# Element-wise sums and products of a fused 256-token network moved from GpSimd to the Vector Engine, in pieces

## The chip, the cores and the metric

The kernel runs on one core of one Trainium2 chip. The core has five engines that work through separate queues of instructions: TensorE for matrix products (PE in the profile; its weight loads are PEld), VectorE (DVE), ScalarE (ACT), GpSimd (POOL) and SyncE (SP), which here only issues DMAs. They wait for each other by semaphores. The metric is the time on the device of one execution, in microseconds (us); lower is better.

## The reference

256 tokens of width 2048 pass through two blocks. The first block is an S5 state-space mixer and a block-sparse attention (NSA), each with a residual and a layer norm; the second block holds two linear recurrences (HGRN2 and a gated delta rule) and a layer of 16384 experts (PEER). Cut to what the change touches:

```python
x = layer_norm(ALPHA * x + s5_mixer(x, ...), ln_g[0], ln_b[0])   # first norm
shared = shared_kv(x, kv_w, ...)                                 # keys, values: x @ kv_w
x = layer_norm(ALPHA * x + nsa_mixer(x, ..., shared), ln_g[1], ln_b[1])   # second norm
xn = _rmsnorm(x, attn_norm_g)
# HGRN2, per chunk: decay between two positions t and s of a chunk
diff = b_c[..., :, None, :] - b_c[..., None, :, :]               # cumulated log decays
att = einsum('bhtd,bhsd,bhtsd->bhts', q_c, k_c, exp(where(causal, diff, -inf)))
h = x + mix @ w_out
hn = _rmsnorm(h, ffn_norm_g)
# PEER, 8 heads
v1, i1 = top_k(s1, 16); v2, i2 = top_k(s2, 16)
cand = v1[..., :, None] + v2[..., None, :]
best, pos = top_k(cand, 16)                                      # pos over the 16 x 16 sums
expert = take_along_axis(i1, pos // 16) * 128 + take_along_axis(i2, pos % 16)
```

## The kernel before, in words

The program is one long chain of stages: `s5`, the first norm (`ln_hat`), `attention`, the second norm (`ln_rms`), `mixers` (gated delta rule and `hgrn`), a third norm (`rms_channels` alone), and `peer`. All weights stream in through one object, `Stream`, in slabs of 128x1024 numbers: SP issues a DMA into one of three `raw` buffers, ACT rounds it to a coarser form `wh` (L152), and a subtraction on DVE yields the rest `wl = raw - wh` (L153). TensorE multiplies the tokens with `wh` and `wl`; three `wh`/`wl` pairs exist. A `wl` that is late stops TensorE. In the first norm's stage a slab feeds 24 products of 256 columns, in `peer` 8 pairs of a 512-column and a 256-column product (tile `pu`).

The order of each engine's queue is fixed when the program is built: a scheduler of the tile framework picks it, and `issue_after(x)` forbids an instruction to stand ahead of x. At run time each queue is worked through in that order, and an instruction that waits holds all behind it.

The places that the change touches:

- First norm. `ln_hat` leaves the normalised tokens both for the product and, in `res`, for the residual. The residual still wants gain and bias: `affine` (L785) multiplies and adds over 128x2048 for each half of the tokens, on POOL (L789, L790), with `gain` (L732) loading both rows from `ln`, spread over 128 partitions. Meanwhile TensorE makes the keys, tile `pk`, eight `kT` tiles, copied out by ACT and DVE by turns (L815).
- Second norm. `ln_rms` applies mean, scale, gain and bias in pieces of 512 columns: five of eight as two DVE instructions (L689, L690), three as ACT Identity (L692) and two POOL instructions (L694, L695). ACT squares each piece, and `rms_channels` scales by the root mean square: half 0 of the tokens on ACT for the first two quarters and DVE for the others (L721, L723), half 1 on DVE (L724). Then TensorE turns the result over (tile `ptc`).
- `rms_channels` also prepares one weight slab on POOL (`prep(2, gpsimd)`) in the second and the third norm.
- `hgrn`. Seven levels l = 6 to 0: differences `E` of the cumulated logs (L1402, POOL, 128x2048), two exponentials on ACT, products with k and q on DVE (L1405, L1406), small matrix products (tile `hp`, L1422), a masked copy into `att` (L1425). TensorE fills the time in between with a projection (tile `pz`).
- `top` finds the best 16 of 128 keys twice per head and forms 16x16 sums, `cand` (L1456, POOL), for a third search on DVE. `routing` compares positions with a ramp (`eq`, L1486, DVE), multiplies with the indices (L1490, POOL, 128x2048) and sums (L1493, DVE). Both run as background steps: one step for every `pu` tile of the expert products.

Of the kernel before, what the change touches and what calls it, by code (L numbers as in the profile page):

```python
# [14 lines left out]
AF = mybir.ActivationFunctionType  # L15
OP = mybir.AluOpType
# [4 lines left out]
T, D = 256, 2048  # L21
# [148 lines left out]
class Kern:  # L170
# [505 lines left out]
    def ln_rms(self, gb, scale):  # L676

        v, act, gp = self.nc.vector, self.nc.scalar, self.nc.gpsimd
        x = self.ln_x
        st = [self.ln_stats(t) for t in range(2)]  # L680
        out = [self.t8([D]) for _ in range(2)]
        sq = self.small.tile([128, 2, 4], F32, name="lnsq")
        behind = lambda n: self.tc.issue_after(n.ins) if n else ExitStack()
        sqr = None
        for t, q in ((0, 0), (0, 1), (0, 2), (1, 0), (0, 3), (1, 1), (1, 2), (1, 3)):
            c = slice(q * 512, q * 512 + 512)
            o = x[t][:, c]
            if q < 2 + t:
                v.scalar_tensor_tensor(o, o, st[t][0], gb[0][:, c], op0=OP.subtract, op1=OP.mult)  # L689
                dve = v.scalar_tensor_tensor(o, o, st[t][1], gb[1][:, c], op0=OP.mult, op1=OP.add)  # L690
            else:
                act.activation(o, o, AF.Identity, scale=st[t][1], bias=st[t][2])  # L692
                with self.tc.issue_after(self.lastpow) if q == 3 else ExitStack():
                    gp.tensor_tensor(o, o, gb[0][:, c], op=OP.mult)  # L694
                    gp.tensor_tensor(o, o, gb[1][:, c], op=OP.add)  # L695
            with behind(sqr):
                sqr = act.activation(out[t][:, c], o, AF.Square, accum_out=sq[:, t, q:q + 1])
        with self.tc.issue_after(self.lastn):
            self.s.prep(1)
        with behind(sqr), behind(dve):  # L700
            return self.rms_channels(x, out, sq, scale)
# [9 lines left out]
    def rms_channels(self, x, out, sq, scale, alloc=None):  # L711
        v, act = self.nc.vector, self.nc.scalar
        r = self.small.tile([128, 2], F32, name="lnrr")
        for t in range(2):
            v.tensor_reduce(r[:, t:t + 1], sq[:, t], axis=AX.X, op=OP.add)
            self.rstd(r[:, t:t + 1], r[:, t:t + 1], 1e-6, 1, 1.0 / D)
        X, pair = self.channels(out, scale, None, alloc)
        for q in range(4):
            c = slice(q * 512, q * 512 + 512)
            if q < 2:  # L720
                act.activation(out[0][:, c], x[0][:, c], AF.Copy, scale=r[:, 0:1])  # L721
            else:
                v.tensor_scalar(out[0][:, c], x[0][:, c], r[:, 0:1], None, op0=OP.mult)  # L723
            v.tensor_scalar(out[1][:, c], x[1][:, c], r[:, 1:2], None, op0=OP.mult)  # L724
            if q == 0:
                self.s.prep(1)
                with self.tc.issue_after(self.lastpow):
                    self.s.prep(2, self.nc.gpsimd)
            self.pairs(X, pair, q)
        return X  # L730

# [50 lines left out]
            fs.append(lambda k: tiles[k // 4][:, k % 4])  # L782
        return tuple(fs), pair

    def affine(self, eng, x, n):  # L785

        gb = self.gain(n)
        for t in range(2):
            eng.tensor_tensor(x[t], x[t], gb[0], op=OP.mult)  # L789
            eng.tensor_tensor(x[t], x[t], gb[1], op=OP.add)  # L790


    def attention(self, res, X):
# [3 lines left out]
        ident, psum, t8 = self.ident, self.psum, self.t8  # L797
        es = ExitStack()
        P = es.enter_context(self.tc.tile_pool(name="att", bufs=1))
        self.affine(gp, res, 0)  # L800
        mk = P.tile([128, 192], F32, name="mk")
        nc.sync.dma_start(mk, i["masks"])
        cp = t8([320])
# [7 lines left out]
        for n in range(8):  # L811
            ps = psum.tile([128, T], F32, tag="mm", name="pk", bufs=2) if n else self.take_first()
            if n:
                self.mm_b(ps, X)
            (act.copy if n % 2 else v.tensor_copy)(kT[:, n % 4, n // 4, :], ps)  # L815
        vv = t8([2, 2, 512])
        for n in range(2):
            pss = [psum.tile([128, 512], F32, tag=("o", "mm")[n], name="pv", bufs=2) for _ in range(2)]
# [97 lines left out]
        for ci in range(12):  # L916
# [7 lines left out]
            st = {}  # L924
# [450 lines left out]
    def hgrn(self, P, qT, kT, bT, vA, OA, lev):  # L1375
# [19 lines left out]
        for l in range(6, -2, -1):  # L1395
            if l >= 0:
# [2 lines left out]
                blk = lambda x: x.rearrange("p h (n w) -> p (h n) w", w=2 * m)  # L1399
                e, k, q = blk(E), blk(kT), blk(qT)  # L1400
                bb = blk(bT)
                gp.tensor_tensor(e, bb, bb[:, :, m - 1:m].to_broadcast(list(bb.shape)), op=OP.subtract)  # L1402
                act.activation(e[:, :, 0:m], e[:, :, 0:m], AF.Exp, scale=-1.0)
                act.activation(e[:, :, m:], e[:, :, m:], AF.Exp)
                v.tensor_tensor(e[:, :, 0:m], e[:, :, 0:m], k[:, :, 0:m], op=OP.mult)  # L1405
# [31 lines left out]
    def top(self, P, x, c, h):  # L1437
# [14 lines left out]
        for a in range(2):  # L1452
            top16(val[:, h, a], idx[:, h, a], x[:, a, :], tl([128], "tmp1", bufs=2))
            yield 1
        cand = tl([16, 16], "cand", bufs=2)
        self.nc.gpsimd.tensor_tensor(cand, val[:, h, 0, :, None].to_broadcast([128, 16, 16]),  # L1456
                                     val[:, h, 1, None, :].to_broadcast([128, 16, 16]), op=OP.add)
        top16(best[:, h], pos[:, h], cand.rearrange("p a b -> p (a b)"), tl([256], "tmp2", bufs=2))
        yield 1

    def routing(self, P, S):
# [6 lines left out]
        for c in range(2):  # L1468
# [12 lines left out]
            for a in range(2):  # L1481
# [3 lines left out]
                for x in range(0, 128, 64):  # L1485
# [1 line left out]
                                    pf[:, a].rearrange("p h s -> p (h s)")[:, x:x + 64, None].to_broadcast([128, 64, 16]),  # L1487
                                    self.iota16[:, None, :].to_broadcast([128, 64, 16]), op=OP.is_equal)
                    yield 1
                gp.tensor_tensor(eq, eq, idf[:, :, a, None, :].to_broadcast([128, 8, 16, 16]), op=OP.mult)  # L1490
                for x in range(0, 128, 64):
                    yield 1
                    v.tensor_reduce(nn[:, a].rearrange("p h s -> p (h s)")[:, x:x + 64], f[:, x:x + 64, :], axis=AX.X,  # L1493
                                    op=OP.add)
# [544 lines left out]
```

## Time and profile before

| | |
|---|---|
| median of 3 runs | 2997.37 us (2997.36 to 3000.99) |
| the profiled execution | 2999.24 us, span 2997.5 us |
| mean granted TensorE clock | 0.969 |
| PE busy | 2842.1 us, 95% of the span |
| DVE, ACT, POOL busy | 66%, 47%, 20% |

The profile is of one execution. Its span runs from the first to the last instruction; the execution's own time is 1.74 us longer. Times in the trace count from the start of the span. The first norm lies at about 290 to 332 us, the second at 988 to 1021, `hgrn` at 1338 to 1430, the third norm at 1560 to 1580, `top` and `routing` at 1600 to 1850.

### The profile page before, as it was taken

The page shows a single profiled execution, that of the slowest core. Times are in us where ns is not written, and L with a number is a line of the kernel's source. Part 1 is how long each engine was busy: PE and PEld are TensorE (multiplying, and loading weights), DVE is VectorE, ACT ScalarE, POOL GpSimd, SP SyncE. Part 2 cuts the span into 40 slices and gives each one's busy share as a digit, 9 for nine tenths or more (in the row PEclk, how much of TensorE's full clock was granted, in tenths as well). Part 3 has the DMA queues.
Part 4 walks back from the last instruction along what each step waited for, and adds up shares of the span by engine and source line. Part 5 has one row for each costly group of instructions (what it writes and reads, how often), then busy time and mean ns, then how long its engine had stood idle before and what let it go on. Part 6 is the DMA issues. An engine that isn't in the chain of part 4 may idle for free. (4 is left out here: it accounts for less than half of the span.)

```text
span 2997.5 us, 44270 instructions
## 1 busy us (share of the span) xinstructions
PE 2842.1 (95%) x17208; PEld 2492.6 (83%) x17212; DVE 1970.3 (66%) x2991; ACT 1415.3 (47%) x1934; POOL 611.2 (20%) x391
## 2 busy tenths in 40 slices
PE   7889899999999799998999999999989998999996
PEld 7888899988878699987878887888878886888884
DVE  8857644555566766448658898777768544777764
ACT  4365333444444557344444444444434443555553
POOL 4360300000000200013000111000000003888882
PEclk9789999999999899999999999999999998999998
DMA  4235554444456454322565556587875767888883
GB/s 172 71 113 172 173 213 161 156 144 138 155 177 217 142 189 141 113 78 99 190 203 181 173 190 222 176 223 223 222 200 185 213 210 268 299 308 317 315 312 149
DMA packets 232097, 569.52 MB, mean 190 GB/s; under 512 B 84257, under 2 KB 117921, under 8 KB 216002
## 3 DMA queue, kind: packets, MB, share of 16 engines
q1 hardware_dynamic: 173986, 411.46, 42.6%
q0 software_dynamic: 23040, 136.46, 12.6%
q10 hardware_dynamic: 34848, 18.62, 2.0%
q8 instruction: 140, 2.29, 0.3%
q14 instruction: 83, 0.68, 0.1%
HBM read 526.89 MB, written 39.59 MB: 189 GB/s over the span
## 5 line engine op out<-in xcount | busy, mean ns | idle before, releaser
L153 DVE TENSOR_TENSOR wl<-raw,wh 128x1024 fp32r<-128x1024 f32 x685 | 883.6, 1292 | 670.3 <-ACT wh L152 669.3
L152 ACT ACTIVATE wh<-raw 128x1024 fp32r<-128x1024 f32 x688 | 727.0, 1058 | 921.1 <-PE pu L225 220.5
L225 PE MATMUL pu<-h,wh 128*128 128x512 f32 x2048 | 735.8, 400 | 4.8 <-DVE qy L1730 2.9
L226 PE MATMUL pu<-h,wl 128*128 128x256 f32 x2048 | 575.5, 281 | 9.4 <-DVE wl L153 9.4
L225 PEld LDWEIGHTS pu<-h,wh 128*128 128x128 f32 x2048 | 386.8, 189 | 96.8 <-DVE w L1902 4.2
L226 PEld LDWEIGHTS pu<-h,wl 128*128 128x128 f32 x2048 | 387.4, 189 | 11.1 <-DVE wl L153 11.1
L241 PE MATMUL pz<-wh,t 128*128 128x512 f32 x1024 | 336.1, 400 | 0.0
L1808 POOL DMA_INDIRECT wg<-WG,idx x107 | 175.6, 1641 | 704.9 <-DVEq L1948 658.5
L1836 PE MATMUL acc<-vwl,hh 128*128 128x512 f32 x644 | 254.0, 394 | 11.9 <-DVE vwl L177 7.1
L1836 PE MATMUL acc<-vwh,hlo 128*128 128x512 f32 x644 | 250.5, 393 | 0.0
L1836 PE MATMUL acc<-vwh,hh 128*128 128x512 f32 x644 | 225.3, 394 | 14.7 <-ACT vwh L176 14.4
L241 PEld LDWEIGHTS pz<-wh,t 128*128 128x128 f32 x1024 | 192.6, 188 | 40.6 <-issue 1.0
L241 PE MATMUL pz<-wl,t 128*128 128x512 f32 x512 | 201.4, 393 | 1.6 <-DVE wl L153 1.4
L241 PE MATMUL pso<-wh,t 128*128 128x512 f32 x640 | 200.7, 393 | 0.4 <-DVE th L1008 0.4
L177 DVE TENSOR_TENSOR vwl<-h,vwh 128x2048 fp32r<-128x2048 f32 x61 | 139.8, 2292 | 39.6 <-ACT vwh L176 36.4
L1836 PEld LDWEIGHTS acc<-vwh,hh 128*128 128x128 f32 x644 | 122.3, 190 | 41.5 <-ACT vwh L176 14.8
L1836 PEld LDWEIGHTS acc<-vwl,hh 128*128 128x128 f32 x644 | 122.6, 190 | 39.2 <-DVE vwl L177 8.3
L1836 PEld LDWEIGHTS acc<-vwh,hlo 128*128 128x128 f32 x644 | 122.7, 190 | 25.6
L241 PEld LDWEIGHTS pso<-wh,t 128*128 128x128 f32 x640 | 120.2, 188 | 26.8 <-DVE th L1008 0.8
L176 ACT ACTIVATE vwh<-h 128x2048 fp32r<-128x2048 f32 x61 | 116.6, 1912 | 48.3 <-DMA h<-pv,idx 47.6
L212 PE MATMUL pq<-t,wh 128*128 128x256 f32 x768 | 138.1, 283 | 0.0
L1903 ACT ACTIVATE w<-w 128x256 f32<-128x256 f32 x128 | 53.4, 417 | 173.0 <-DVE w L1902 173.0
(621 smaller groups left out, 5325.0 us busy)
## 6 DMA issues: line engine op xcount, KB each, us to landing
raw<-pu SPq DMA_DIRECT2D x256, 512.0 KB, 4.1
raw<-w_z SPq DMA_DIRECT2D x96, 512.0 KB, 3.3
raw<-w_fqi SPq DMA_DIRECT2D x48, 512.0 KB, 3.3
raw<-w_a_in SPq DMA_DIRECT2D x32, 512.0 KB, 3.3
raw<-w_q SPq DMA_DIRECT2D x32, 512.0 KB, 3.3
raw<-w_b_out SPq DMA_DIRECT2D x32, 512.0 KB, 3.9
raw<-w_conv SPq DMA_DIRECT2D x32, 512.0 KB, 3.6
raw<-w_gz SPq DMA_DIRECT2D x32, 512.0 KB, 3.3
```

The source lines that it names most:

```text
L152: self.nc.scalar.activation(h, t, AF.Copy)
L153: m = (engine or self.nc.vector).tensor_tensor(l, t, h.bitcast(F32), op=OP.subtract).ins
L176: self.nc.scalar.activation(h, x, AF.Copy)
L177: (engine or self.nc.vector).tensor_tensor(l, x, h.bitcast(F32), op=OP.subtract)
L212: mm = nc.tensor.matmul(ps, a[:, c], b(k), start=(k == 0 and n == 0), stop=(k == nk - 1 and n == len(ops) - 1))
L225: nc.tensor.matmul(ps, w[0][:, c], x[2](k), start=k == 0, stop=False, skip_group_check=True)
L226: mm = nc.tensor.matmul(ps[:, 0], w[1][:, c], x[0](k), start=False, stop=k == nk - 1, skip_group_check=True)
L241: self.nc.tensor.matmul(pss[tt], x[a](k)[:, ts], b[:, kk * 512:(kk + 1) * 512], start=(k == 0 and n == 0), stop=(k == nk - 1 and n == 2))
L1808: gp.indirect_dma_start(out=g.rearrange("p a b t -> p (a b t)"), out_offset=None, in_=wghalf if a else wgrows, in_offset=off(0))
L1836: m = pe.matmul(acc[t][e], a[:, k], b[:, es], start=start and n == 0, stop=True, skip_group_check=True)
L1903: act.activation(w1, w1, AF.Gelu)
```

## The change

What POOL did in these places is done by DVE, mostly in smaller pieces. In the second norm all eight pieces are DVE pairs, in the order of the tokens' halves, and ACT's Identity goes too. In `rms_channels` ACT scales all of half 0, and the slab that POOL prepared is DVE's. `affine` becomes a generator that does 512 columns of one half per step, one step behind each `kT` tile, not ahead of the last weight slab prepared by then; the loads of gain and bias are issued with the first step; ACT copies all eight `kT` tiles. `hgrn`'s difference is two DVE instructions of 128x1024 per level, `cand` one of 128x256, and the product of `eq` with the indices two of 128x1024, each ahead of a background step.

```diff
@@ ln_rms
-        for t, q in ((0, 0), (0, 1), (0, 2), (1, 0), (0, 3), (1, 1), (1, 2), (1, 3)):
+        for t, q in ((t, q) for t in range(2) for q in range(4)):
             c = slice(q * 512, q * 512 + 512)
             o = x[t][:, c]
-            if q < 2 + t:
-                v.scalar_tensor_tensor(o, o, st[t][0], gb[0][:, c], op0=OP.subtract, op1=OP.mult)
-                dve = v.scalar_tensor_tensor(o, o, st[t][1], gb[1][:, c], op0=OP.mult, op1=OP.add)
-            else:
-                act.activation(o, o, AF.Identity, scale=st[t][1], bias=st[t][2])
-                with self.tc.issue_after(self.lastpow) if q == 3 else ExitStack():
-                    gp.tensor_tensor(o, o, gb[0][:, c], op=OP.mult)
-                    gp.tensor_tensor(o, o, gb[1][:, c], op=OP.add)
+            v.scalar_tensor_tensor(o, o, st[t][0], gb[0][:, c], op0=OP.subtract, op1=OP.mult)
+            dve = v.scalar_tensor_tensor(o, o, st[t][1], gb[1][:, c], op0=OP.mult, op1=OP.add)
@@ rms_channels
-            if q < 2:
-                act.activation(out[0][:, c], x[0][:, c], AF.Copy, scale=r[:, 0:1])
-            else:
-                v.tensor_scalar(out[0][:, c], x[0][:, c], r[:, 0:1], None, op0=OP.mult)
+            act.activation(out[0][:, c], x[0][:, c], AF.Copy, scale=r[:, 0:1])
...
-                    self.s.prep(2, self.nc.gpsimd)
+                    self.s.prep(2)
@@ affine
-    def affine(self, eng, x, n):
+    def affine(self, x, n):
         gb = self.gain(n)
-        for t in range(2):
-            eng.tensor_tensor(x[t], x[t], gb[0], op=OP.mult)
-            eng.tensor_tensor(x[t], x[t], gb[1], op=OP.add)
+        for c in range(0, D, 512):
+            for t in range(2):
+                o = x[t][:, c:c + 512]
+                for g, op in zip(gb, (OP.mult, OP.add)):
+                    self.nc.vector.tensor_tensor(o, o, g[:, c:c + 512], op=op)
+                yield 1
@@ attention
-        self.affine(gp, res, 0)
+        quarters = self.affine(res, 0)
...
-            (act.copy if n % 2 else v.tensor_copy)(kT[:, n % 4, n // 4, :], ps)
+            act.copy(kT[:, n % 4, n // 4, :], ps)
+            with self.tc.issue_after(s.last):
+                next(quarters)
@@ hgrn
-                gp.tensor_tensor(e, bb, bb[:, :, m - 1:m].to_broadcast(list(bb.shape)), op=OP.subtract)
+                nb = 128 // m
+                for x in range(0, 8 * nb, 4 * nb):
+                    r = slice(x, x + 4 * nb)
+                    v.tensor_tensor(e[:, r], bb[:, r], bb[:, r, m - 1:m].to_broadcast([128, 4 * nb, 2 * m]),
+                                    op=OP.subtract)
@@ top
-        self.nc.gpsimd.tensor_tensor(cand, val[:, h, 0, :, None].to_broadcast([128, 16, 16]),
-                                     val[:, h, 1, None, :].to_broadcast([128, 16, 16]), op=OP.add)
+        v.tensor_tensor(cand, val[:, h, 0, :, None].to_broadcast([128, 16, 16]),
+                        val[:, h, 1, None, :].to_broadcast([128, 16, 16]), op=OP.add)
@@ routing
-                gp.tensor_tensor(eq, eq, idf[:, :, a, None, :].to_broadcast([128, 8, 16, 16]), op=OP.mult)
                 for x in range(0, 128, 64):
+                    h4 = slice(x // 16, x // 16 + 4)
+                    v.tensor_tensor(eq[:, h4], eq[:, h4], idf[:, h4, a, None, :].to_broadcast([128, 4, 16, 16]),
+                                    op=OP.mult)
                     yield 1
```

How the queues move is shown at three places, in the order in which the engine works; L numbers of the changed kernel are its own.

DVE's queue in the first norm, before: `t_2420` is the last operand of the first key products, `pfirst` and `pk` are key tiles.

```order
L153 TENSOR_TENSOR wl<-raw,wh 128x1024
L778 TENSOR_TENSOR t_2420<-t_2416,t_2418 128x512
L153 TENSOR_TENSOR wl<-raw,wh 128x1024
L815 COPY t_2577<-pfirst 128x256
L153 TENSOR_TENSOR wl<-raw,wh 128x1024 x3
L815 COPY t_2577<-pk 128x256
```

The same place after; `t_1777` and `t_1778` are the halves of the residual, `t_2571` and `t_2572` the loaded gain and bias.

```order
L153 TENSOR_TENSOR wl<-raw,wh 128x1024
L769 TENSOR_TENSOR t_2420<-t_2416,t_2418 128x512
L153 TENSOR_TENSOR wl<-raw,wh 128x1024 x3
L783 TENSOR_TENSOR t_1777<-t_1777,t_2571 128x512
L783 TENSOR_TENSOR t_1778<-t_1778,t_2571 128x512
L783 TENSOR_TENSOR t_1777<-t_1777,t_2572 128x512
L783 TENSOR_TENSOR t_1778<-t_1778,t_2572 128x512
L153 TENSOR_TENSOR wl<-raw,wh 128x1024
```

The copies have left DVE's queue; four of the sixteen short instructions stand behind the third `wl` after the operand, and further `wl` slabs behind them. On SP the two loads of `ln` stood ahead of `cmp` and of the seventh `raw` of these weights; now:

```order
L798 DMA t_2563<-cmp 128x320
L140 DMA raw<-w_kT 128x1024
L726 DMA t_2571<-ln 128x2048
L726 DMA t_2572<-ln 128x2048
L140 DMA raw<-w_kT 128x1024 x9
```

They are behind a `raw` that waits for a buffer.

DVE's queue near the end of `hgrn`, after, for the levels 2 to 0 (`t_12069`, `t_12132`, `t_12195` are their `E`, `t_9711` the cumulated logs; L1401 is the moved difference):

```order
L1401 TENSOR_TENSOR t_12132<-t_9711 128x1024 x2
L153 TENSOR_TENSOR wl<-raw,wh 128x1024 x2
L1401 TENSOR_TENSOR t_12195<-t_9711 128x1024 x2
L1405 TENSOR_TENSOR t_12132<-t_12132,t_9712 128x512x2
L1406 TENSOR_TENSOR t_12132<-t_12132,t_9713 128x512x2
L1405 TENSOR_TENSOR t_12195<-t_12195,t_9712 128x1024
L1406 TENSOR_TENSOR t_12195<-t_12195,t_9713 128x1024
```

Before, no L1401 stood there; two slabs and four L1405/L1406 came directly behind each other. The level-1 products now have both slabs and the level-0 difference ahead of them.

DVE's queue in `routing`, after (L1492 is the product with the indices, L1495 the sum):

```order
L1904 TENSOR_TENSOR w<-w,pu 128x256
L1492 TENSOR_TENSOR eq<-eq,idf 128x1024
L153 TENSOR_TENSOR wl<-raw,wh 128x1024
L1495 TENSOR_REDUCE nn<-eq 128x64
L1492 TENSOR_TENSOR eq<-eq,idf 128x1024
L1904 TENSOR_TENSOR w<-w,pu 128x256
L153 TENSOR_TENSOR wl<-raw,wh 128x1024
```

Before, these rows stood there without the two of the product, which was one instruction on POOL.

## Rows read from the trace of the kernel before

**Rows 1.** The page: busy time, share and instructions by engine.

```profile
PE 2842.1 (95%) x17208; PEld 2492.6 (83%) x17212; DVE 1970.3 (66%) x2991; ACT 1415.3 (47%) x1934; POOL 611.2 (20%) x391
```

**Rows 2.** One of POOL's groups by line: busy, mean ns of one, idle before.

```profile
L1402 POOL TENSOR_TENSOR t<-t 128x2048 f32<-128x2048 f32 x7 | 28.5, 4095 | 15.7 <-PE hp L1422 9.5 <-PE hps L1391 5.1 <-issue 1.1
```

**Rows 3.** POOL's timeline in the first norm: start, duration, instruction.

```profile
307.44 10.01 POOL L789 TENSOR_TENSOR t<-t,t 128x2048 f32<-128x2048 f32 x2
```

**Rows 4.** DVE's timeline in the first norm: start, duration, instruction, idle before.

```profile
307.95 5.15 DVE L153 TENSOR_TENSOR wl<-raw,wh 128x1024 fp32r<-128x1024 f32 x1 [0.99 <-ACT wh L152]
313.02 4.98 DVE L778 TENSOR_TENSOR t<-t,t 128x512 fp32r<-128x512 f32 x1
...
333.50 1.23 DVE L153 TENSOR_TENSOR wl<-raw,wh 128x1024 fp32r<-128x1024 f32 x1 [1.17 <-ACT wh L152]
```

**Rows 5.** PE's waits, 306 to 333 us: total, times, longest.

```profile
PE pk L212 <- DVE wl L153: 6.5, 3, 3.1
PE pfirst L185 <- DVE t L778: 4.4, 1, 4.4
```

**Rows 6.** Windows: length, busy (instructions) by engine, clock, DMA share, GB/s.

```profile
308.00:332.00 24.00, 13.14 (x94) 12.34 (x93) 23.40 (x8) 4.50 (x5) 19.94 (x4) 0.86 0.21 68
344.00:352.00 8.00, 8.00 (x73) 8.00 (x73) 3.51 (x4) 3.44 (x4) 0.00 (x0) 1.00 0.58 194
```

**Rows 7.** DMA issues at 296 to 300 us: KB each, median us to landing.

```profile
t<-ln SPq DMA_DIRECT2D x2, 1024.0 KB, 6.7
```

**Rows 8.** PE's waits, 985 to 1025 us.

```profile
PE ptc L754 <- ACT t L721: 15.7, 1, 15.7
```

**Rows 9.** DVE's timeline in the second norm.

```profile
989.73 0.74 DVE L689 SCALAR_TENSOR_TENSOR t<-t,bnmv,t 128x512 f32<-128x512 f32 x1
...
991.65 2.42 DVE L690 SCALAR_TENSOR_TENSOR t<-t,lnr,t 128x512 f32<-128x512 f32 x2
...
998.78 3.42 DVE L690 SCALAR_TENSOR_TENSOR t<-t,lnr,t 128x512 f32<-128x512 f32 x2
1002.13 1.75 DVE L689 SCALAR_TENSOR_TENSOR t<-t,bnmv,t 128x512 f32<-128x512 f32 x1
```

**Rows 10.** PE's waits in `hgrn`, 1334 to 1392 us.

```profile
PE hps L1391 <- DVE t L1386: 6.8, 1, 6.8
PE pz L241 <- DVE wl L153: 1.4, 1, 1.4
```

**Rows 11.** DVE's timeline in `hgrn`.

```profile
1341.27 2.23 DVE L1382 TENSOR_TENSOR t<-t 128x1024 f32<-128x1024 f32 x1
1343.42 4.72 DVE L153 TENSOR_TENSOR wl<-raw,wh 128x1024 fp32r<-128x1024 f32 x1
1348.06 2.27 DVE L1217 TENSOR_REDUCE hss<-t 128x16 f32<-128x2048 f32 x1
...
1384.07 2.32 DVE L1406 TENSOR_TENSOR t<-t,t 128x1024 f32<-128x1024 f32 x1
```

**Rows 12.** One window, most of `hgrn`.

```profile
1340.00:1390.00 50.00, 40.47 (x230) 35.00 (x230) 43.41 (x36) 32.23 (x33) 31.77 (x9) 0.93 0.19 64
```

**Rows 13.** PE's waits in the third norm, 1560 to 1580 us.

```profile
PE ptc L754 <- DVE t L724: 5.4, 1, 5.4
```

**Rows 14.** Windows over the searches and `routing`.

```profile
1700.00:1720.00 20.00, 20.00 (x115) 17.25 (x114) 18.86 (x21) 8.16 (x13) 5.97 (x2) 1.00 0.61 182
...
1700.00:1850.00 150.00, 139.14 (x756) 118.59 (x755) 139.80 (x300) 68.68 (x100) 28.71 (x12) 0.97 0.58 185
```

**Rows 15.** DVE's groups by line, 1700 to 1850 us.

```profile
L153 DVE TENSOR_TENSOR wl<-raw,wh 128x1024 fp32r<-128x1024 f32 x47 | 73.5, 1568 | 5.0 <-ACT wh L152 4.7
L1902 DVE TENSOR_TENSOR w<-w,pu 128x256 f32<-128x256 f32 x24 | 9.8, 409 | 0.8 <-ACT w L1901 0.7
L1486 DVE TENSOR_TENSOR eq<-pf,iotaf 128x1024 f32<-128x1024 f32 x8 | 9.7, 1221 | 0.1
```

**Rows 16.** PE's waits, 1680 to 1860 us.

```profile
PE pu L226 <- DVE wl L153: 8.9, 3, 3.8
```

## The prediction

> **What bounds the kernel now.** Read first the page's busy times by engine: TensorE works for 2842.1 of 2997.5 us, so at most some 155 us of waiting can be won anywhere, and DVE with 66% and POOL with 20% look harmless [rows 1]. That average hides what matters: the waits for DVE lie in a few stretches. So the next view is TensorE's waits, stretch by stretch, and then DVE's timeline in each of them.
>
> In the first norm the product waits 6.5 us for `wl` and 4.4 us for the last operand, both made by DVE [rows 5]. DVE's timeline shows why. The same subtraction that takes 1.23 us at 333.50 takes 5.15 us at 307.95, and a 128x512 one behind it takes 4.98 us [rows 4]. POOL begins its two long multiplications at 307.44 and is done with them 10.01 us later, some 5 us each [rows 3]: the first ends near 312.45, DVE's row ends at 313.10. Each DVE row lasts until a POOL instruction is done. I read that as DVE's two-operand instructions standing still while POOL works on two operands. The same pattern shows in `hgrn`, where at 1343.42 a subtraction takes 4.72 us beside POOL's level differences, while a plain sum over 128x2048 at 1348.06 takes 2.27 us [rows 2, 11]; and in `routing`, where the mean `wl` takes 1568 ns [rows 15].
>
> **The change, stage by stage.** Prices on DVE: a 128x1024 two-operand instruction is 1.22 us [rows 15], a row ends 0.08 us behind the start of the next [rows 4], so each added one costs 1.14 us of the queue. By the same 0.08 a 128x512 one costs 0.66 [rows 9], and a 128x256 one, like `cand`, 0.33 [rows 15].
>
> *First norm.* Of 24 us TensorE is busy 13.14; it does 94 products where the undisturbed stretch does 73 in 8 us [rows 6]. The idle time alone is 10.9 us; by the count (94 at 9.13 per us are 10.3 us) the stretch loses 13.7. The granted clock is 0.86 there [rows 6], so part of the difference is products at the lower level; I take 12.4 lost. The sixteen new pieces cost DVE 16 x 0.66 = 10.6 us over eight key tiles, some 22 us, in which an undisturbed DVE is busy 3.51 of 8 us [rows 6] and so has about 12 us of room; that room hides them, and if it were gone each us would be TensorE's. New is a wait for the loads. They now stand on SP behind a `raw` whose buffer is freed by the `wl` of 307.95, which undisturbed ends near 309.2; landing takes 6.7 us [rows 7], so gain and bias arrive at 316 to 318. The first four pieces are queued behind the third `wl` after the operand, which I put at 315, with the next `wl` behind them. TensorE wants that one near 320.4: from the operand at 309.9, four slabs of 24 products at 0.11 us lie ahead of it. The loads at 316 to 318, four pieces (2.6 us) and the slab (1.1) end at 320 to 322, so it nearly fits; I charge 0.6. Gain 11.8, between 8 (loads 4 us later) and 13.7.
>
> *Second norm.* One gap, 15.7 us before the first turned-over tile [rows 8], is DVE's chain. Three pairs move to it: six instructions, 4.0 us. Gone are the stalls beside POOL: the pairs at 991.65 and 998.78 take 2.42 and 3.42 where 1.4 is normal, the next instruction 1.75 where 0.74 is [rows 9], 4.0 together. DVE's part then ends when it did, or up to 1 us earlier if the rows between had stalls too; the slab that POOL prepared and the scalings that ACT takes over shorten what follows by 1 to 2. I take 2.3, between 0.5 and 3.5.
>
> *hgrn.* In 50 us TensorE is busy 40.47 [rows 12], 8.2 of the loss in two waits [rows 10]; with the clock at 0.93 [rows 12] I take 11 lost. DVE's seven overlong rows, from the 2.23 at 1341.27 to the 2.32 at 1384.07 [rows 11], hold about 16.3 us beyond their normal lengths; the last of them is beside a POOL product that stays, so 15.1 go. Added are 14 x 1.14 = 16.0. DVE's 43.41 busy us [rows 12] become 44.3, against the 39 that TensorE would need: DVE is now what bounds the stage. Packed without a hole it gives 50 - 44.3 = 5.7. With as many holes as before (6.6) it gives nothing, and one more spell at the lower clock costs about 2. The early wait of 6.8 goes, because the differences of the lower levels come after it; near the end level 1's products stand behind two slabs and level 0's difference, and their matrix products will wait some 4 to 5 us. I take 3.5, between -2 and 5.7.
>
> *Third norm.* The wait of 5.4 us for the half that DVE scales [rows 13] runs beside the one slab that POOL prepared; that slab now costs DVE 1.14 instead. I take 1.1, between 0 and 2.
>
> *Searches and routing.* In 150 us TensorE is idle 10.9 and at a mean clock of 0.97; it does 756 products where the first 20 us do 115 [rows 14], which by the count is 18.4 us lost. The idle time with the slow spells behind it comes to nearer 16; I take 16.5. The waits named are 8.9 us for `wl` [rows 16]. The 47 `wl` rows hold 47 x (1.568 - 1.222) = 16.3 us of stall [rows 15]. Added are eight products, 9.1 us, and eight of the sixteen `cand`, 2.6 (the other eight fall in 1600 to 1700, where I charge nothing): 11.8. DVE's 139.8 busy us [rows 14] become 135.3, TensorE's need is 133.5. Packed perfectly that gives 14.7; DVE's waits for ACT's `wh`, 5.0 us [rows 15], will in part stay, so I let the stage take 139. Gain 11, between 5 and 14.7.
>
> The Trainium skill (Perfetto Trace Analysis, Optimizing Scalar/DVE Operations) speaks against this stage: where DVE is saturated, work may be given away, even to GpSimd, though between those two it might not help. By that rule a DVE at 139.8 of 150 us that takes 11.8 more would use up its 10.2 us of holes and end 1.6 us later, and the sum would be 17 instead of 30.
>
> **Sum.** 11.8 + 2.3 + 3.5 + 1.1 + 11 = 29.7 us. The profiled execution took 2999.24 us, so it would take 2969.5; the median of the runs is 1.9 lower, which puts the new median at 2967.7, say **2968 us**. TensorE's work after 1850 us only moves forward.
>
> **Rivals.**
>
> *DVE becomes the bound.* Both `hgrn` and `routing` are left with a DVE as long as the stage. If its holes stay, `hgrn` gives -1 and `routing` 5: the sum is 19, the time 2978. For it: 44.3 against 39, and 135.3 against 133.5. Against: the holes were partly made by TensorE itself being late.
>
> *The stalls are not POOL's.* The rows show coincidence; no row names POOL as what holds DVE. If DVE is slow there for a reason of its own, only work is added: 16.0 less 6.6 of holes in `hgrn`, 11.8 less 10.2 in `routing`, 4.0 in the second norm, and 10.6 in a first norm where DVE is busy 23.40 of 24 us [rows 6]. That is 25 us more, about 3022. It decides from the point where less than half of the stall time disappears. Against it: DVE's long rows end where POOL's do, and the same forms run at 1.23 elsewhere [rows 3, 4].
>
> *Nothing to see.* If the stalls go but the added work takes their place nearly one for one, as 15.1 against 16.0 in `hgrn`, everywhere, the gain is under 6 us: about 2994.
>
> *The whole loss comes back.* Upper ends of all stages: 13.7 + 3.5 + 5.7 + 2 + 14.7 = 40, so 2958.
>
> **Chances and range.** The forecast 0.53, DVE as bound 0.25, the whole loss back 0.14, nothing to see 0.05, stalls not POOL's 0.03. The range takes in the first three with their unknowns: 2955 to 2984 us. A measurement of this kernel tells a change from none at about 0.2%, 6 us. Faster than that holds in the first three cases: 0.92; within it 0.05; slower 0.03.
>
> **What would show it.** Right: `wl` rows of 1.2 us in all four stretches; no wait above 1 us in the first norm; the wait at the second norm near 14; `hps` waiting under 2 us and a new wait of 4 to 5 at `hp` near the end of `hgrn`; in `routing` no `wl` wait of 3.8 and DVE busy nearly throughout. Wrong: the first L783 far behind 318 us, with `wl` behind it (loads too late); `hp` waits of 10 us together; or `wl` still at 5 us with POOL idle.

## The result and the profile after

The changed kernel takes 2966.86 us (median of 4 runs, 2961.79 to 2970.22) against 2997.41 of the kernel before, measured beside it: a ratio of 0.9893, 95% interval 0.9878 to 0.9909. The profiled execution took 2967.33 us with a span of 2965.6, 31.9 us less than the profiled one of before.

The page's busy times of the changed kernel: POOL lost 104 us of work, DVE, which took it over, is 15 us *less* busy than in [rows 1].

```profile
PE 2842.4 (96%) x17212; PEld 2494.9 (84%) x17212; DVE 1955.0 (66%) x3045; ACT 1420.0 (48%) x1941; POOL 507.1 (17%) x352
```

**Where the time came from.** The same products of TensorE mark the same points in both traces (the timeline's first or last row of a tile). Their distances, in us:

| stretch | before | after | gained |
|---|---|---|---|
| start to first `pfirst` (S5, not touched) | 297.0 | 294.6 | 2.4 |
| to first `pv` (first norm, keys) | 61.9 | 49.7 | 12.2 |
| to last `pso` (attention) | 632.7 | 632.7 | 0.0 |
| to first `pgc` (second norm) | 41.5 | 38.9 | 2.6 |
| to first `pz` on the gated-delta outputs (not touched) | 191.5 | 189.9 | 1.6 |
| to last `pso` of the second block (`hgrn`, output) | 339.7 | 341.1 | -1.4 |
| to first `pu` (third norm, queries) | 110.7 | 110.0 | 0.7 |
| to last `prt` (searches, routing) | 176.5 | 163.0 | 13.5 |
| to the last `acc` | 1129.2 | 1128.9 | 0.3 |

Within the sixth row, `hgrn` itself (to its last `hps`) goes from 205.5 to 208.0; the output product behind it gets 1.1 us back.

**First norm.** DVE's timeline in the changed kernel, start, duration, instruction, idle before, against [rows 4]:

```profile
305.18 1.22 DVE L153 TENSOR_TENSOR wl<-raw,wh 128x1024 fp32r<-128x1024 f32 x1 [0.75 <-ACT wh L152]
306.32 0.68 DVE L769 TENSOR_TENSOR t<-t,t 128x512 fp32r<-128x512 f32 x1
...
312.81 1.29 DVE L783 TENSOR_TENSOR t<-t,t 128x512 f32<-128x512 f32 x2
316.27 1.29 DVE L783 TENSOR_TENSOR t<-t,t 128x512 f32<-128x512 f32 x2 [2.16 <-DMA t<-ln]
318.63 1.23 DVE L153 TENSOR_TENSOR wl<-raw,wh 128x1024 fp32r<-128x1024 f32 x1 [1.07 <-ACT wh L152]
```

The subtraction of 5.15 us is 1.22, the operand of 4.98 is 0.68. The loads, 1024 KB each, come in at 312.8 and 316.2, and two pieces wait 2.16 us for the second of them. The slab behind costs TensorE the only wait left there, but it does not wait for the pieces: DVE is done with them at 317.56 and then idle for 1.07 us, until ACT has rounded that slab. ACT in turn waits for the slab's `raw`, which SP issued behind the two loads and which landed 7.9 us after its issue (8.0 and 7.2 for the next two, 3.9 for the one ahead of the loads). ACT's timeline, PE's waits, 300 to 333 us, and the window of [rows 6]:

```profile
317.54 1.06 ACT L152 ACTIVATE wh<-raw 128x1024 fp32r<-128x1024 f32 x1 [1.18 <-DMA raw<-w_kT]
```

```profile
PE pk L212 <- DVE wl L153: 0.8, 1, 0.8
```

```profile
308.00:332.00 24.00, 23.24 (x200) 22.96 (x199) 17.17 (x20) 11.18 (x15) 0.00 (x0) 1.00 0.79 279
```

TensorE does 200 products where it did 94, at the upper clock throughout.

**Second norm.** PE's wait of 15.7 us [rows 8] is 13.8, and DVE's rows have their normal length, where [rows 9] had 3.42 and 1.75:

```profile
PE ptc L745 <- ACT t L714: 13.8, 1, 13.8
```

```profile
983.02 1.41 DVE L689 SCALAR_TENSOR_TENSOR t<-t,lnr,t 128x512 f32<-128x512 f32 x2
984.35 1.41 DVE L688 SCALAR_TENSOR_TENSOR t<-t,bnmv,t 128x512 f32<-128x512 f32 x2
```

**hgrn.** The waits of [rows 10] are gone; one of 4.6 us is new, at the level-1 products. PE's waits, PE's timeline from level 2 to level 0, and two windows (busy by engine, then the clock):

```profile
PE hp L1422 <- DVE t L1406: 5.9, 2, 4.6
```

```profile
1376.63 3.76 PE L1422 MATMUL hp<-t 128*128 128x64 f32 x32 [1.24 <-DVE t L1406]
...
1391.41 10.47 PE L1422 MATMUL hp<-t 128*128 128x64 f32 x48 [4.61 <-DVE t L1406]
...
1401.89 3.51 PE L1422 MATMUL hp<-t 128*128 128x64 f32 x16
```

```profile
1390.00:1400.00 10.00, 8.59 (x41) 8.62 (x41) 6.96 (x11) 4.53 (x5) 1.28 (x1) 0.50 0.00 0
1400.00:1410.00 10.00, 10.00 (x52) 9.44 (x52) 6.82 (x9) 0.00 (x0) 0.00 (x0) 0.64 0.01 2
```

Level 2 does 32 products in 3.76 us. Behind the wait the granted clock is 0.50, the lower of its two levels (1.2 and 2.4 GHz), and 64 products take 14.0 us instead of 7.5. DVE's timeline ahead of that wait shows what stands between:

```profile
1381.04 2.34 DVE L1401 TENSOR_TENSOR t<-t 128x1024 f32<-128x1024 f32 x2
1383.30 2.35 DVE L153 TENSOR_TENSOR wl<-raw,wh 128x1024 fp32r<-128x1024 f32 x2
1385.57 3.42 DVE L1401 TENSOR_TENSOR t<-t 128x1024 f32<-128x1024 f32 x2
1388.92 1.21 DVE L1405 TENSOR_TENSOR t<-t,t 128x1024 f32<-128x1024 f32 x1
1390.05 1.21 DVE L1406 TENSOR_TENSOR t<-t,t 128x1024 f32<-128x1024 f32 x1
```

**Third norm.** The wait of 5.4 us [rows 13] is 3.3:

```profile
PE ptc L745 <- DVE t L715: 3.3, 1, 3.3
```

**Searches and routing.** PE's waits for `wl`, the window from first `pu` to last `prt`, and DVE's `wl` rows there, against [rows 14 to 16]:

```profile
PE pu L226 <- DVE wl L153: 0.9, 3, 0.4
```

```profile
1657.00:1820.00 163.00, 161.70 (x911) 139.43 (x911) 149.98 (x362) 81.41 (x116) 0.00 (x0) 0.99 0.63 196
```

```profile
L153 DVE TENSOR_TENSOR wl<-raw,wh 128x1024 fp32r<-128x1024 f32 x54 | 65.6, 1214 | 8.6 <-ACT wh L152 8.2
```

A slab takes 1.21 us instead of 1.57, DVE is 92% busy, and TensorE waits 0.9 us for it in all.

### The profile page after: what moved, and what is told of

The parts are those of the page before. It is cut to its first block, busy times and chain, and to the rows that moved or that the text cites. A ratio compares the mean times of both kernels' runs of the same rounds, so it can differ in the third digit from the quotient of the medians.

```text
span 2965.6 us, 44243 instructions
## 1 busy us (share of the span) xinstructions
PE 2842.4 (96%) x17212; PEld 2494.9 (84%) x17212; DVE 1955.0 (66%) x3045; ACT 1420.0 (48%) x1941; POOL 507.1 (17%) x352
## 3 DMA queue, kind: packets, MB, share of 16 engines
q8 instruction: 140, 2.29, 0.3%
## 5 line engine op out<-in xcount | busy, mean ns | idle before, releaser
L153 DVE TENSOR_TENSOR wl<-raw,wh 128x1024 fp32r<-128x1024 f32 x687 | 852.0, 1242 | 648.7 <-ACT wh L152 646.5
L1810 POOL DMA_INDIRECT wg<-WG,idx x107 | 182.7, 1708 | 701.8 <-DVEq L1950 656.8
L177 DVE TENSOR_TENSOR vwl<-vraw,vwh 128x2048 fp32r<-128x2048 f32 x48 | 110.0, 2292 | 28.6 <-ACT vwh L176 28.4
```

Source lines behind the costliest of these rows:

```text
L153: m = (engine or self.nc.vector).tensor_tensor(l, t, h.bitcast(F32), op=OP.subtract).ins
L177: (engine or self.nc.vector).tensor_tensor(l, x, h.bitcast(F32), op=OP.subtract)
L1810: gp.indirect_dma_start(out=g.rearrange("p a b t -> p (a b t)"), out_offset=None, in_=wghalf if a else wgrows, in_offset=off(0))
```

## The experiments

What has to be told apart: whether GpSimd's *reading* is what holds DVE (theory 1) or DVE was slow there for its own reasons; whether the piece's length or the engine matters; and what `hgrn` lost. Other parts of the program vary by several us between executions (the S5 start takes 289.5 to 298.8, the stretch of the `acc` products 469.5 to 479.4), so single runs are judged by the stretches, which repeat within 1.4 us in the attention, 1.2 in the first norm and 2 in routing where the code is the same. `hgrn` as changed repeats only within 4. Here are the stretches of all runs, `hgrn` to its last `hps` and, in brackets, with the output product:

| run | first norm | routing | `hgrn` | whole, us (runs) | ratio to before |
|---|---|---|---|---|---|
| before | 61.9 | 176.5 | 205.5 (339.7) | 2997.41 (4) | 1 |
| after | 49.7 | 163.0 | 208.0 (341.1) | 2966.86 (4) | 0.9893 |
| e1 `hgrn` on GpSimd | 50.0 | 161.7 | 205.4 (339.6) | 2974.58 (1) | |
| e2 two levels ahead | 50.9 | 161.7 | 206.9 (339.9) | 2963.93 (4) | 0.9889 (0.9861 to 0.9916) |
| e3 unused products | 50.3 | 176.7 | 208.3 (341.4) | 2985.78 (1) | |
| e4 unused fills | 50.0 | 164.0 | 211.9 (344.9) | 2969.86 (1) | |
| e5 gain and bias pieces on GpSimd | 49.8 | 163.5 | 208.6 (341.7) | 2971.11 (1) | |
| e6 routing halves on GpSimd | 50.7 | 176.4 | 211.9 (344.9) | 2988.97 (1) | |
| e7 two parts alone | 49.7 | 163.4 | 205.0 (339.2) | 2972.04 (4) | 0.9919 (0.9889 to 0.9948) |
| e8 e2, early loads | 47.9 | 161.8 | 206.9 (340.2) | 2962.01 (5) | 0.9881 (0.9860 to 0.9901) |
| e9 held back | 48.0 | 161.8 | 211.9 (346.6) | 2970.43 (6) | 0.9911 (0.9890 to 0.9931) |
| e10 held back, halves | 48.1 | 161.8 | 209.0 (343.2) | 2968.08 (4) | 0.9900 (0.9876 to 0.9923) |
| e11 levels split | 48.7 | 161.8 | 210.3 (343.4) | 2964.24 (4) | 0.9891 (0.9869 to 0.9913) |
| e12 e1, early loads | 48.2 | 161.7 | 205.4 (339.6) | 2962.06 (6) | 0.9894 (0.9871 to 0.9916) |

**e3: GpSimd reads, for nothing.** Added to the changed kernel, behind each conversion of the indices; DVE's queue is word for word the same:

```diff
+            junk = tl([8, 16, 16], "junk")
+            gp.tensor_copy(junk[:, 0, 0], idf[:, 0, 0])
+            for a in range(2):
+                b = idf[:, :, a, None, :].to_broadcast([128, 8, 16, 16])
+                gp.tensor_tensor(junk, b, b, op=OP.mult)
```

> The changed kernel, with GpSimd given four two-operand 128x2048 products in routing whose results nobody uses, some 18 us in all, two behind each conversion of the indices; DVE's own instructions and their order are unchanged. Theory 1 (a GpSimd instruction that reads two operands stops DVE's two-operand instructions for its length): wl rows of 3 to 6 us beside them, PE waits for wl again, the stretch from the first pu product to the last turned-over gate tile, 163.0 us in the changed kernel and 176.5 before, grows by 6 to 16 us, the whole to 2973 to 2983. Rival (DVE was slow there before for a reason of its own): wl rows stay at 1.2 us, the stretch at 162 to 164, the whole at 2967.

The stretch is 176.7 us, 13.7 more: all that the change had won there is lost again to work that nobody uses. The whole, 2985.8, lies 3 above the stated span; S5 and the gated delta rule, which the edit doesn't touch, took 2.7 and 2.1 us more in that run. DVE's timeline behind the first conversion, and GpSimd's (two products of 4.1 us each):

```profile
1691.83 4.50 DVE L1491 TENSOR_TENSOR eq<-pf,iotaf 128x1024 f32<-128x1024 f32 x1
1696.26 4.62 DVE L153 TENSOR_TENSOR wl<-raw,wh 128x1024 fp32r<-128x1024 f32 x1
1700.80 1.21 DVE L1491 TENSOR_TENSOR eq<-pf,iotaf 128x1024 f32<-128x1024 f32 x1
```

```profile
1691.60 8.19 POOL L1485 TENSOR_TENSOR junk<-idf 128x2048 f32<-128x2048 f32 x2
```

Each of the first two rows lasts until just after a product is done (1695.7 and 1699.8); the row that follows has its 1.21 us again. Groups by line over the stretch, DVE's and then GpSimd's:

```profile
L153 DVE TENSOR_TENSOR wl<-raw,wh 128x1024 fp32r<-128x1024 f32 x51 | 68.4, 1341 | 4.2 <-ACT wh L152 3.8
L1491 DVE TENSOR_TENSOR eq<-pf,iotaf 128x1024 f32<-128x1024 f32 x8 | 16.2, 2054 | 0.1
```

```profile
L1485 POOL TENSOR_TENSOR junk<-idf 128x2048 f32<-128x2048 f32 x4 | 17.2, 4290 | 0.3
```

**e4: GpSimd writes as long.** The same place, with the loop replaced:

```diff
-            for a in range(2):
-                b = idf[:, :, a, None, :].to_broadcast([128, 8, 16, 16])
-                gp.tensor_tensor(junk, b, b, op=OP.mult)
+            for a in range(5):
+                gp.memset(junk, 0.0)
```

> As the run with four unused products on GpSimd, but with ten fills of 128x2048 in their place, about 18 us as well, which write and read nothing. Theory 1 (reading is what collides): wl rows stay at 1.2 us beside the fills, the stretch at 162 to 165 us, the whole at 2965 to 2969. Rival (any work of GpSimd on the same memory stops DVE): the stretch grows as much as with the products, 6 to 16 us.

The stretch is 164.0 (the whole, 2969.9, 0.9 above the stated span), and DVE's rows are as in the changed kernel although GpSimd works just as long:

```profile
L153 DVE TENSOR_TENSOR wl<-raw,wh 128x1024 fp32r<-128x1024 f32 x49 | 59.5, 1214 | 2.4 <-ACT wh L152 2.0
```

```profile
L1484 POOL MEMSET junk<- 128x2048 f32 x10 | 18.3, 1832 | 0.6
```

So what holds DVE's two-operand instructions is neither that GpSimd is busy nor that it writes. The products read and multiply, the fills do neither; that it is the reading, these two runs alone don't tell. The Trainium skill (SBUF — State Buffer, Who interferes with whom) says it so: a DVE instruction with two SBUF inputs contends with a GpSimd instruction that reads SBUF, not with one that only writes, and the later of the two waits for the whole of the other. e3 and e4 agree, and so does the sum over one operand in [rows 11]: 2.27 us beside GpSimd's differences, 2.29 in the changed kernel without them.

**e5: short pieces on GpSimd, first norm.**

```diff
-                    self.nc.vector.tensor_tensor(o, o, g[:, c:c + 512], op=op)
+                    self.nc.gpsimd.tensor_tensor(o, o, g[:, c:c + 512], op=op)
```

> The changed kernel with the sixteen gain and bias pieces of 128x512 given to GpSimd, same pieces, same places. The stretch from the first pfirst product to the first pv product is 49.7 us in the changed kernel and 61.9 before. Theory 1 (a two-operand row of DVE waits for the GpSimd instruction that is running, so at most some 1.3 us for a piece): wl rows of up to 2.5 us, which DVE's slack in this stage mostly covers; the stretch is 50 to 55 us, the whole 2967 to 2972. Rival (what counts is how long GpSimd works in all, some 20 us, however it is cut): the stretch is 58 to 62 us, the whole 2975 to 2980.

49.8 us: as good as on DVE. The pieces take 29.9 us of GpSimd, more than the 20.5 of the four long ones, and `wl` rows grow to 1.59 us, but DVE is idle enough:

```profile
L783 POOL TENSOR_TENSOR t<-t,t 128x512 f32<-128x512 f32 x16 | 29.9, 1907 | 7.6 <-issue 7.6
```

```profile
L153 DVE TENSOR_TENSOR wl<-raw,wh 128x1024 fp32r<-128x1024 f32 x15 | 23.7, 1592 | 15.4 <-ACT wh L152 13.9 <-issue 1.4
```

**e6: short pieces on GpSimd, routing.**

```diff
-                    v.tensor_tensor(eq[:, h4], eq[:, h4], idf[:, h4, a, None, :].to_broadcast([128, 4, 16, 16]),
-                                    op=OP.mult)
+                    gp.tensor_tensor(eq[:, h4], eq[:, h4], idf[:, h4, a, None, :].to_broadcast([128, 4, 16, 16]),
+                                     op=OP.mult)
```

> The changed kernel with the eight 128x1024 products of routing given to GpSimd, each ahead of the same background step; the 16x16 sums stay on DVE. The stretch from the first pu product to the last turned-over gate tile is 163.0 us in the changed kernel, 176.5 before. Theory 1 (each GpSimd piece holds up the next two-operand row of DVE for its own length, and here DVE has no slack to cover it): wl rows of 2 to 3.5 us, PE waits for wl, the stretch 168 to 176 us, the whole 2972 to 2980. Rival (short pieces are what matters, on whichever engine): the stretch 162 to 165 us, the whole 2966 to 2969.

176.4 us, as before the change and 0.4 over theory 1's upper end: cutting in halves won nothing, although here the small sums are on DVE, which before were on GpSimd too. Both sides are held up: `wl` and `eq` rows on DVE, and GpSimd's halves, which take 3.05 us where the whole one took 4.81. (The whole, 2989, is above both spans; the other stretches of that run were long too.)

```profile
L153 DVE TENSOR_TENSOR wl<-raw,wh 128x1024 fp32r<-128x1024 f32 x52 | 73.0, 1408 | 6.4 <-ACT wh L152 5.7
L1486 DVE TENSOR_TENSOR eq<-pf,iotaf 128x1024 f32<-128x1024 f32 x8 | 16.3, 2048 | 0.1
```

```profile
L1492 POOL TENSOR_TENSOR eq<-eq,idf 128x1024 f32<-128x1024 f32 x8 | 24.4, 3054 | 231.8 <-DVE eq L1486 231.8
```

With e5 this answers the question of length in part. Where DVE has room, short pieces behind the key tiles are enough and the engine doesn't matter; whether it is their length or their later places, no run separates, since none has the long instructions in the new places. Where DVE is full, cutting didn't help: by the rows above the eight pieces cost DVE 10.1 us in `wl` and 6.6 in `eq`, 2.1 a piece, and doing the work itself costs it 1.14.

**e7: the two large parts alone.** The kernel before, with the diff's `affine`, `attention`, `top` and `routing` and nothing else.

> The kernel before with only two parts of the change: gain and bias in pieces on DVE, and the sums and products of the searches and routing on DVE; both norms behind it and hgrn as before. Theory 1 (these two carry the gain, 12 and 13 us in the trace of the changed kernel; hgrn gives nothing back and the norms 3): 2968 to 2973 us, 25 to 29 faster than before and 0 to 4 slower than the changed kernel. Rival (the parts help each other, or hgrn's move pays in another place): 2975 or more.

2972.0 us, 24.9 less than the kernel before measured beside it: at the edge of theory 1's span. Against the changed kernel it is 5.2 us slower, a little more than the 0 to 4 stated; the intervals of the two ratios overlap. The stretches repeat (49.7, 163.4) and `hgrn` keeps 205.0. The second norm takes 42.0 against 38.9 and the third, with the queries, 111.8 against 110.0, which is what their parts of the change are worth here.

**e1 and e2: what hgrn lost.** e1 puts the difference back as one `gp.tensor_tensor` per level; e2 leaves it on DVE, two levels ahead (`diff(l)`, whose definition is cut here, does the two instructions of a level):

```diff
...
+        ready = [diff(l) for l in range(6, 6 - 2, -1)]
         for l in range(6, -2, -1):
             if l >= 0:
                 m = 2 ** l
-                E = t8([8, T])
+                if l >= 2:
+                    ready.append(diff(l - 2))
+                E = ready.pop(0)
```

> The changed kernel with the level differences of hgrn back on GpSimd, one 128x2048 instruction per level. In the trace of the changed kernel the stretch from the first pz product on the gated-delta outputs to the last hps product of hgrn is 208.0 us, before the change it was 205.5. Theory 1 (the move of hgrn lost there, the rest of the gain is elsewhere): the stretch comes back to 205 to 206, the two-operand rows of DVE are overlong again at its beginning, and the whole is 2 to 3 us faster than the changed kernel, about 2964. Rival (the later end came from another part of the change or from a different state of the clock): the stretch stays at 207 to 209 or the whole stays at 2967.

> The changed kernel with the level differences of hgrn still on DVE, each issued two levels ahead of its use, so that none stands directly ahead of the products of levels 1 and 0. Theory 1 (what hgrn lost was the order at the end of the stage: 4.6 us of waiting at hp, and some 7.5 us of products at the lower clock behind it): no wait above 1 us at hp for level 1, no spell at half clock, the stretch of 208.0 us falls to 195 to 198, the whole to 2954 to 2957. Rival (DVE has too much work in this stage, in whatever order): the waits move to other levels or to wl, the stretch stays at 204 to 208, the whole at 2963 to 2967.

e1's stretch is 205.4, and its waits are those of the kernel before again, the 6.8 and 1.4 us of [rows 10] and one of 1.2. DVE's overlong rows are back too; its timeline beside GpSimd's first four differences:

```profile
1329.14 4.72 DVE L153 TENSOR_TENSOR wl<-raw,wh 128x1024 fp32r<-128x1024 f32 x1
1333.79 2.27 DVE L1213 TENSOR_REDUCE hss<-t 128x16 f32<-128x2048 f32 x1
...
1338.50 3.78 DVE L618 TENSOR_SCALAR rs_a<-hss 128x16 f32<-128x16 f32 x1
```

```profile
1324.49 17.75 POOL L1398 TENSOR_TENSOR t<-t 128x2048 f32<-128x2048 f32 x4
```

In the changed kernel these three rows take 1.22, 2.29 and 0.17 us. So two operands are not a condition: the tiny TENSOR_SCALAR has one, is held for 3.6 us and ends with GpSimd's fourth difference, at 1342.3.

e1's one whole run, 2974.6, is not 2964; the last stage was 5 us longer and S5 2 us, which the edit doesn't touch. Over all runs `hgrn` takes 205.0 to 205.5 us with the differences on GpSimd in whole instructions and not held back (four traces), and 208.0 to 211.9 on DVE as changed (five). So this part of the change costs 2.5 us or more, of which the next product gives 1.1 back.

e2 met half of its theory. Level 1 waits no more, but the stretch is 206.9, not 195 to 198; PE's timeline shows what took the place:

```profile
1388.06 3.68 PE L1429 MATMUL hp<-t 128*128 128x64 f32 x32
...
1394.90 6.45 PE L1429 MATMUL hp<-t 128*128 128x64 f32 x32 [2.28 <-DVE t L1413]
```

Now level 0 waits, 2.3 us, and again at the lower clock behind it (6.45 us for 32 products); another 1.8 us wait is at level 5. The stretch and the whole, 2963.9, are those of the rival, too much work for DVE in whatever order.

**e9 to e11: other orders and splits.** e9 makes GpSimd start behind the first operand, by a copy of one number ahead of its fill; e10 does so in halves; e11 leaves levels 6 to 3 on DVE. All have the early loads of e8.

```diff
+        gp.tensor_copy(att[:, 0, 0, 0:1], E[:, 0, 128:129])
         gp.memset(att, 0.0)
```

> The changed kernel with the early loads of gain and bias, and with the level differences of hgrn on GpSimd in whole 128x2048 instructions as before the change, but held back: a copy of one number from the operand of the first hps products makes GpSimd start only when DVE has finished that operand. In the traces so far hgrn's stretch (first pz product on the gated-delta outputs to last hps product) is 205.0 to 205.5 us with the differences on GpSimd, 206.9 on DVE two levels ahead, 208.0 to 211.9 on DVE as changed. Theory 1 (on GpSimd the loss is the 6.8 us wait for that operand, made by overlong DVE rows beside GpSimd's first four differences): the wait goes, no spell at half clock follows it, and the stretch is 196 to 200 us unless wl rows become late, the whole 2954 to 2958. Rival (DVE's rows are held up just as long afterwards, and TensorE waits there): 203 to 207, the whole 2961 to 2966.

> As the run with the differences held back on GpSimd, in fourteen 128x1024 pieces. Theory 1 (a DVE row waits for one GpSimd instruction, so a shorter one costs a row less, where DVE has slack): the stretch is equal to that of the whole instructions or up to 3 us shorter. Rival (as in routing, halves cost as much as wholes, since DVE's next row meets the next piece): equal or longer by up to 3 us.

> The changed kernel with the early loads, and with hgrn's differences on DVE for levels 6 to 3 and on GpSimd, in halves, for levels 2 to 0. Theory 1 (with the change hgrn loses at its end, where DVE has to do the differences of levels 1 and 0 beside two slabs; these are now off DVE): no wait of 4.6 us at hp for level 1 and no long spell at half clock, the stretch 198 to 203 us, the whole 2956 to 2961. Rival (GpSimd's reads stop DVE as long as DVE's own differences took): a wait of 3 us or more stays, the stretch 205 to 210 us.

e9's stretch is 211.9, 12 above its theory and above the rival's 207 too, and so is its whole, 2970.4. e10's is 209.0, 2.9 shorter than e9's: theory 1, at its outer end. e11's is 210.3 with a long wait, as its rival has it; the whole, 2964.2, is above theory 1. In e9 the early wait is gone and one of 7.9 us at `hp` has come; in e10 and e11 the longest is for `wl`. PE's waits in `hgrn`, e9:

```profile
PE hp L1418 <- DVE t L1402: 10.2, 2, 7.9
```

and e11:

```profile
PE pz L241 <- DVE wl L153: 7.1, 1, 7.1
```

In none of these forms is the stage shorter than with GpSimd let free, and the waits alone don't say why. Windows over the stretch, of the kernel before, the changed one and e9 (length, busy by engine, clock):

```profile
1224.60:1430.10 205.50, 195.84 (x1291) 176.19 (x1289) 117.97 (x130) 82.99 (x92) 37.29 (x12) 0.98 0.28 93
```

```profile
1205.80:1413.80 208.00, 201.50 (x1299) 182.21 (x1298) 119.39 (x144) 86.07 (x94) 8.32 (x5) 0.96 0.28 92
```

```profile
1201.60:1413.50 211.90, 201.68 (x1286) 182.52 (x1286) 126.13 (x130) 83.44 (x92) 40.28 (x13) 0.94 0.27 90
```

TensorE is idle for 9.7 us in the kernel before, 6.5 in the changed one and 10.2 in e9; the mean granted clock is 0.98, 0.96 and 0.94. So the changed kernel waits less than the one before and loses by slower products, and e9 waits about as long as the one before and loses in the same way; e2, e10 and e11 have 0.96, 0.96 and 0.95. That DVE and GpSimd together have too much work between the first operand and the last level fits the waits that only move, but is argued, not shown by a run.

**e8 and e12: the best versions.** The loads are issued ahead of the key tiles again:

```diff
-        quarters = self.affine(res, 0)
+        quarters = self.affine(res, self.gain(0))
```

with `affine` taking the two tiles. e8 adds this to e2, e12 to e1.

> The changed kernel with two repairs: hgrn's differences two levels ahead, as in the run before, and the loads of gain and bias issued ahead of the key tiles, as they were before the change. Theory 1: the wait of 0.8 us in the first norm goes, hgrn's stretch is 205 to 207 us instead of 208, the whole 2962 to 2965. Rival (neither repair shows beside the spread of the runs): 2965 to 2969.

> The version that the stretches so far point to: the changed kernel with hgrn's differences back on GpSimd as before the change (205.0 to 205.5 us in three traces against 208.0 to 211.9 in five on DVE) and the loads of gain and bias ahead of the key tiles (first norm 47.9 to 48.7 us against 49.7). Theory 1: the two add up, hgrn's stretch 205 to 206, the first norm 48, the whole 4 to 6 us below the changed kernel, 2960 to 2964, a ratio of 0.987 to 0.989 to the kernel before. Rival (other stretches, which vary by 5 us from run to run, hide it): the stretches as said, the whole 2964 to 2970.

The first norm takes 47.9 and 48.2 us, 1.5 to 1.8 less than in the changed kernel, and no wait for `wl` is left in it; `hgrn` is as expected in both. The wholes are 2962.0 and 2962.1, but their ratios (0.9881 and 0.9894) overlap with that of the changed kernel, 0.9893. Both beat the kernel before clearly; that they beat the changed one is shown by the stretches only, not by the whole.

## Why the prediction was right, point by point

It forecast 2968 us, 2955 to 2984, and 2966.86 came. The sum was right to 1 us; its terms were not all.

- *The mechanism.* Read from coincidence in [rows 3, 4, 11]; e3 and e4 show it in routing, e1 in `hgrn`, where the rows come and go with GpSimd's work. "Two-operand" was too narrow, as the TENSOR_SCALAR of e1 shows. The rival that the stalls were DVE's own is refuted: DVE's rows are 1.21 us once GpSimd's reading instructions are gone, and in the first norm and routing the added work is covered.
- *First norm, 11.8.* Measured 12.2. The 6.7 us to landing was the median of two loads; the second, issued at 307.3, was there at 316.2, 8.9 later, and DVE's pieces waited 2.16 us for it. Charged 0.6, TensorE's wait was 0.8, which is luck in part: it was charged to the pieces ahead of the slab, and came from the slab's own `raw`, which had to follow the loads. e8 and e12 show what that place was worth in all, 1.5 to 1.8.
- *Second norm, 2.3.* Measured 2.6, with a wait of 13.8 where near 14 was named.
- *Third norm, 1.1.* Measured 0.7 with the queries behind it.
- *Searches and routing, 11.* Measured 13.5. The step that was off is the one that let the stage take 139 of 150 us, 5.5 more than TensorE needs, for DVE's holes. Charging most of the wait for ACT's `wh` was too much: TensorE waits 0.9 us for `wl`, and against a need of 160 us (176.5 less the 16.5 taken as lost) the stretch loses 3.0. The rule of the Trainium skill that was weighed there (Perfetto Trace Analysis, Optimizing Scalar/DVE Operations) would have had the stretch 1.6 us longer; the trace has it 13.5 shorter, since the work that was off-loaded cost the saturated engine more than doing it. The Trainium skill's own reserve there, that between these two engines it might not help, is what came out.
- *hgrn, 3.5.* Measured -1.4, the one step of wrong sign, within its bounds of -2 to 5.7. The wait at level 1 was named as 4 to 5 us and is 4.6, and the wait of 6.8 went. The term that was mis-sized is the clock: "costs about 2" for one more spell, for which no row was given, where 64 products behind the wait took 6.5 us more than at the upper level. TensorE's idle time did fall, from 9.7 to 6.5 us. (DVE's seven overlong rows held 15.8 us beyond their lengths, not 16.3, which changes little.) The lower bound, a DVE that keeps its holes and one more spell, was the better guide: e2 and e9 to e11 moved the loss about and never got below 205.

The misses have opposite signs, and stretches that nothing touched were 4.0 us shorter in that trace (S5 and the gated delta rule): the exact hit of the whole owes something to that. The five terms together came to 27.6 us, against 29.7 forecast.

## What to carry to other kernels

Look for rows of one form with two durations. If the long ones end where another engine's instruction ends, price the off-loaded work at what it takes from the engine it was to relieve: in routing 28.7 us of GpSimd's products and small sums [rows 14] held DVE up for some 16 us, and doing them costs DVE 12. Cut the pieces short where the held engine has room, and take the work back where it has none. And price a gap of TensorE with the slow spell that follows it, which here cost 6.5 us against the gap's 4.6.

## What the runs showed that was not expected

- Pieces on GpSimd are slowed too: 128x512 ones took 1.91 us beside DVE (e5) where 1.28 was the mean of others of that size, and 128x1024 ones 3.05 (e6) where a whole 128x2048 one took 4.81.
- After the TensorE wait of 4.6 us in `hgrn` the granted clock was 0.50 until about 1407 us. In five traces of the same code the stretch is near 208 in three and 211.9 in two, e4 and e6. In these two the clock was at its lower level once more ahead of that wait, behind the 1.2 us wait at level 2, where the changed kernel had 1.00 all the way to 1390. Why it fell there in two traces and not in the other three stays open. Windows in e4 and then in the changed kernel, clock third from the end of each line:

```profile
1378.00:1384.00 6.00, 6.00 (x24) 5.42 (x24) 3.17 (x4) 0.00 (x0) 0.00 (x0) 0.50 0.50 165
1391.00:1411.00 20.00, 17.57 (x76) 16.93 (x77) 13.78 (x19) 5.84 (x6) 1.27 (x1) 0.50 0.00 1
```

```profile
1365.00:1390.00 25.00, 19.91 (x120) 16.75 (x118) 22.80 (x21) 13.80 (x14) 1.75 (x1) 1.00 0.39 126
1391.00:1407.00 16.00, 15.59 (x71) 15.42 (x72) 9.78 (x16) 3.53 (x4) 1.28 (x1) 0.50 0.00 0
```

- `hgrn` in its held-back forms is longer by 3.6 to 6.5 us than with GpSimd let free although TensorE is idle hardly longer in them (10.1 and 10.2 us against 9.7); the difference is mostly the lower clock. Why it stays low for longer there is open too.
